# Loads of adaLN weights moved from SyncE's queue to ScalarE's, beside the first FFN product

## The chip, the cores and the metric

The kernel runs on one core of a Trainium2 chip. A core has TensorE (PE, matrix products), VectorE (DVE), ScalarE (ACT), GpSimd (POOL) and SyncE (SP). Each engine works through its own instructions in order and waits for the others on semaphores; 16 DMA engines move data between HBM and on-chip memory. A transfer is started by an instruction on some engine, in that engine's order. The metric is the device time of one execution in microseconds (us), lower is better.

## What is computed

The reference is a two-layer backbone over 1024 latent tokens and 256 context tokens of width 1024. Each layer mixes tokens (attention, long convolution, mLSTM) and then applies a SwiGLU FFN of width 2816. Both are modulated by vectors from a linear map of the condition (adaLN):

```python
for l in range(DEPTH):                                   # DEPTH = 2
    mod = (s_lat @ w_mod[l] + b_mod[l])[:, None, :]       # shift, scale, gate: 6 x 1024 values
    mod_c = s_ctx @ w_mod[l] + b_mod[l]
    ...
    x = x + g1 * y                                        # y: the token mixer
    x = x + g2 * swiglu(modulate(x, norm2_w[l], sh2, sc2), ffn_w_gate[l], ffn_w_up[l], ffn_w_down[l])
    if not last:
        ctx = ctx + g1c * yc
        ctx = ctx + g2c * swiglu(modulate(ctx, ...), ...)
```

## The kernel before, in words

All weights and activations are float32. For TensorE every operand is split in two parts: ScalarE writes a rounded copy ("hi", L137) and VectorE the remainder ("lo", L142), and a product is made of three matmuls: hi by hi, hi by lo, lo by hi.

The stage that the change touches is the first FFN product of layer 0 (`second` calls `up`). It makes gate and up values for 2816 features in 11 pairs of 128-feature blocks, and each pair takes two passes (i = 0 gate, i = 1 up). One such pass, called a step here, computes a 256-feature by 1024-token product with seven half-size products instead of eight (`products`, in the manner of Strassen and Winograd). There are 22 steps. A step's matmuls are 84 of 512 columns (into the PSUM tiles a, b, c, d, lines L1239 to L1241, `partial`) and 48 of 256 columns for the context tokens (into x, lines L169 to L171, the helper `rest` in `up`).

A step needs weights prepared by `up_weights`. Two loads of 512 KB each bring `raw` tiles: one with the quarters A11 and A12, the other with A21 and A22. GpSimd makes four sums of quarters from them (S1, S3, S2, S4, L1176); S1 and S3 need the second tile. ScalarE and VectorE then split the four quarters and the four sums into hi and lo (eight L137 and eight L142 instructions of 128x512). There are two `raw` buffers in all, so a step's loads can start only when the previous step's quarters have been split, and there is one set of split weights, so a split must also wait until TensorE has finished with that tile in the previous step. While TensorE works on a step, the other engines prepare the next one and finish the results of the current one: VectorE combines PSUM tiles (w, y, p, L1176; y is the one that reads b when its second half is done), ScalarE copies (p, L1253 and L1258) and applies SiLU (g), and results go out to `act`.

Beside this stage the kernel makes the rest of the adaLN vectors (`late_mod`), woven into the 22 steps: 160 times a tile `mraw` of 256 KB of adaLN weights is loaded, and one VectorE instruction multiplies it by the SiLU of the condition and sums it (L1739 before, L1737 after; CUSTOM_DVE_ANT_0 in the profile, ISA in the program's rows). There are three `mraw` buffers, so a load waits for the VectorE instruction three tiles earlier. About 7.3 of these fall on a step.

A scheduler sets the order of instructions on each engine, from its own estimate. Tokens constrain it: instructions stamped with one token stay in program order. Before, all loads are issued by SyncE, and the loads of `raw` in the FFN and of `mraw` bear the token "queue".

Of the kernel before, what the change touches and what calls it, by code (L numbers as in the profile page):

```python
# [83 lines left out]
class Kernel:  # L84
# [1190 lines left out]
    def up_weights(self, l, f, i, sp, full):  # L1275

        nc = self.nc
        G = nc.gpsimd
        q, w = {}, {}
        for r in "12":  # L1280
            t = self.t(self.wp, [P, 1024], F32, "raw", 2)
            ins = nc.sync.dma_start(out=t, in_=self.A["wgu"][l, f + int(r) - 1, i])
            self.tc.stamp_issue_order_token(ins.ins, "queue")
            q["A" + r + "1"], q["A" + r + "2"] = t[:, :512], t[:, 512:]
        for x in (("S3", "S4"), ("A11", "A12"), ("S1", "S2"), ("A22", "A21")):
            hi, lo = [self.t(self.wl, [P, 1024], F32R, "w", 8) for _ in range(2)]
            for i, y in enumerate(x):
                w[y] = hi[:, i * 512:(i + 1) * 512], lo[:, i * 512:(i + 1) * 512]
        As, Ss = ("A11", "A12", "A22") + (("A21",) if full else ()), ("S3", "S4", "S1", "S2")
        if sp is None:  # L1290
            for x in As:
                self.split(*w[x], q[x])
            for x, y in (("S1", "A22"), ("S3", "A21"), ("S2", "A11"), ("S4", "A12")):
                q[x] = q[y]
            order = Ss
        else:
            for x in (("S3", "S4"), ("S1", "S2")):
                t = self.t(sp, [P, 1024], F32, "S", bufs=2)
                q[x[0]], q[x[1]] = t[:, :512], t[:, 512:]
            order = Ss[:2] + As[:2] + Ss[2:] + As[2:]  # L1300
        for x, y, z, op in (("S1", "A21", "A22", ALU.add), ("S3", "A11", "A21", ALU.subtract), ("S2", "S1", "A11", ALU.subtract),
                            ("S4", "A12", "S2", ALU.subtract)):
            self.tt(G, q[x], q[y], q[z], op)
        for x in order:
            self.split(*w[x], q[x])
        return w
# [416 lines left out]
    def late_mod(self, mr):  # L1723

        nc = self.nc
        H = DM // 2
        for v, n in ((0, 48), (1, 16)):
            for h in range(2):
                cs = slice(h * H, (h + 1) * H)
                sil = self.t(mr, [P, H], F32, "silb", 1)  # L1730
                nc.sync.dma_start(out=sil, in_=self.A["crow"][v, cs].partition_broadcast(P))
                nc.scalar.activation(out=sil, in_=sil, func=AF.Silu)
                for l, f in [(0, f) for f in range(40, 48)] + [(1, f) for f in range(n)]:
                    d = self.L[l]
                    raw = self.t(mr, [P, H], F32, "mraw", 3)
                    ins = nc.sync.dma_start(out=raw, in_=self.A["wmodT"][l, f][:, cs])
                    self.tc.stamp_issue_order_token(ins.ins, "queue")  # L1737
                    o = d["mod"][:, f, v:v + 1]
                    ins = nc.vector.tensor_tensor_reduce(out=raw, in0=raw, in1=sil, scale=1.0, scalar=o if h else d["bmod"][:, f:f + 1],  # L1739
                                                         op0=ALU.mult, op1=ALU.add, accum_out=o)  # L1740
                    self.tc.stamp_issue_order_token(ins.ins, "pace")
                    yield
# [113 lines left out]
```

## Time and profile before

| what | before |
|---|---|
| device time, median of 3 runs | 3420.31 us (3418.61 to 3427.58) |
| the profiled execution's own time | 3420.54 us |
| its span, first to last instruction | 3418.4 us |
| mean granted TensorE clock | 0.963 of full speed |
| TensorE busy | 3191.8 us, 93% of the span |
| VectorE busy | 2137.8 us, 63% |
| ScalarE busy | 1283.5 us, 38% |
| GpSimd busy | 871.1 us, 25% |
| share of the 16 DMA engines that SyncE's queue took | 41.8% |
| first and last issue of an `mraw` load | 1005.8 us, 1555.1 us |

Times of single instructions are counted from the span's start. A matmul's record overlaps the next one's, so the distance between starts, not the length, is its cost.

### The profile page before, as it was taken

The page shows a single profiled execution, that of the slowest core. Times are in us where ns is not written, and L with a number is a line of the kernel's source. Part 1 is how long each engine was busy: PE and PEld are TensorE (multiplying, and loading weights), DVE is VectorE, ACT ScalarE, POOL GpSimd, SP SyncE. Part 2 cuts the span into 40 slices and gives each one's busy share as a digit, 9 for nine tenths or more (in the row PEclk, how much of TensorE's full clock was granted, in tenths as well). Part 3 has the DMA queues.
Part 4 walks back from the last instruction along what each step waited for, and adds up shares of the span by engine and source line. Part 5 has one row for each costly group of instructions (what it writes and reads, how often), then busy time and mean ns, then how long its engine had stood idle before and what let it go on. Part 6 is the DMA issues. An engine that isn't in the chain of part 4 may idle for free. (4 is left out here: it accounts for less than half of the span.)

```text
span 3418.4 us, 48478 instructions
## 1 busy us (share of the span) xinstructions
PE 3191.8 (93%) x17486; PEld 2737.4 (80%) x17486; DVE 2137.8 (63%) x3929; ACT 1283.5 (38%) x2775; POOL 871.1 (25%) x800
## 2 busy tenths in 40 slices
PE   7998999988979999998999999999899699999998
PEld 3976898887868778787888897899887578887787
DVE  8678457895587766664554755456885844444443
ACT  5544466444352222222221642456344533333210
POOL 2354133111133333332000230133112444443000
PEclk8999999998989999999999999999899899999999
DMA  6676446442624444445331465445336122223432
GB/s 235 204 221 207 121 128 188 138 115 78 199 70 136 139 139 134 157 132 173 106 92 56 131 207 172 129 125 179 102 91 199 62 74 84 77 84 103 159 99 74
DMA packets 350319, 454.48 MB, mean 133 GB/s; under 512 B 48064, under 2 KB 250740, under 8 KB 348287
## 3 DMA queue, kind: packets, MB, share of 16 engines
q1 hardware_dynamic: 349704, 451.05, 41.8%
q8 instruction: 138, 2.26, 0.3%
q14 instruction: 102, 0.84, 0.1%
q10 hardware_dynamic: 375, 0.34, 0.0%
HBM read 335.10 MB, written 116.16 MB: 132 GB/s over the span
## 5 line engine op out<-in xcount | busy, mean ns | idle before, releaser
L137 ACT ACTIVATE w<-raw 128x512 fp32r<-128x512 f32 (+3 forms) x286 | 220.9, 798 | 398.8 <-PE f L170 129.2
L169 PE MATMUL f<-b,w 128*128 128x512 f32 (+1 forms) x912 | 335.3, 377 | 30.9 <-ACT b L137 29.8
L142 DVE TENSOR_TENSOR w<-raw,w 128x512 fp32r<-128x512 f32 (+3 forms) x266 | 268.2, 1025 | 144.9 <-ACT w L137 143.1
L170 PE MATMUL f<-b,w 128*128 128x512 f32 (+1 forms) x912 | 332.7, 366 | 0.0
L171 PE MATMUL f<-b,w 128*128 128x512 f32 (+1 forms) x912 | 331.9, 365 | 0.0
L1374 DVE SCALAR_TENSOR_TENSOR x<-f,mod,x 128x512 f32<-128x512 f32 (+1 forms) x256 | 168.5, 664 | 194.7 <-PE f L171 189.4
L169 PE MATMUL mm<-w,hh 128*128 128x256 f32 (+2 forms) x928 | 279.3, 302 | 9.4 <-ACT hh L315 5.1
L171 PE MATMUL mm<-w,hl 128*128 128x256 f32 (+2 forms) x928 | 276.7, 300 | 5.4 <-DVE hl L316 5.4
L170 PE MATMUL mm<-w,hh 128*128 128x256 f32 (+2 forms) x928 | 277.6, 299 | 1.2 <-DVE w L142 1.2
L142 DVE TENSOR_TENSOR w<-S,w 128x512 fp32r<-128x512 f32 x168 | 136.9, 835 | 155.0 <-ACT w L137 148.1
L169 PEld LDWEIGHTS f<-b,w 128*128 128x128 f32 x912 | 176.1, 195 | 63.5 <-ACT b L137 32.4
L137 ACT ACTIVATE w<-S 128x512 fp32r<-128x512 f32 x168 | 100.5, 624 | 335.0 <-POOL S L1176 331.7
L170 PEld LDWEIGHTS f<-b,w 128*128 128x128 f32 x912 | 175.4, 192 | 29.1 <-DVE b L142 1.0
L171 PEld LDWEIGHTS f<-b,w 128*128 128x128 f32 x912 | 175.0, 192 | 26.5
L169 PEld LDWEIGHTS mm<-w,hh 128*128 128x128 f32 x928 | 178.2, 192 | 14.7 <-ACT hh L315 7.2
L171 PEld LDWEIGHTS mm<-w,hl 128*128 128x128 f32 x928 | 177.1, 192 | 7.3 <-DVE hl L316 6.8
L170 PEld LDWEIGHTS mm<-w,hh 128*128 128x128 f32 x928 | 178.4, 192 | 1.9 <-DVE w L142 1.6
L1239 PE MATMUL d<-hb,w 128*128 128x512 f32 x352 | 142.2, 404 | 15.2 <-ACT w L137 7.7
L1176 POOL TENSOR_TENSOR S<-raw 128x512 f32<-128x512 f32 x42 | 56.1, 1336 | 388.6 <-DMA raw<-in_wgu 328.4
L1241 PE MATMUL b<-hb,w 128*128 128x512 f32 x352 | 139.1, 395 | 12.6 <-DVE w L142 12.6
L1241 PE MATMUL d<-hb,w 128*128 128x512 f32 x352 | 142.6, 405 | 8.9 <-DVE w L142 8.7
L1240 PE MATMUL a<-hb,w 128*128 128x512 f32 x352 | 139.7, 397 | 7.9 <-DVE hb L142 7.8
(697 smaller groups left out, 8815.1 us busy)
## 6 DMA issues: line engine op xcount, KB each, us to landing
raw<-in_wgu SPq DMA_DIRECT2D x88, 512.0 KB
mraw<-in_wmodT SPq DMA_DIRECT2D x160, 256.0 KB
act<-g SPq DMA_DIRECT2D x88, 256.0 KB
raw<-in_wdn SPq DMA_DIRECT2D x44, 512.0 KB
raw<-act SPq DMA_DIRECT2D x42, 512.0 KB
raw<-in_wout SPq DMA_DIRECT2D x32, 512.0 KB
q<-qd SPq DMA_DIRECT2D x144, 96.0 KB
eoL<-eo SPq DMA_DIRECT2D x64, 192.0 KB
```

What stands on the lines that cost most here:

```text
L137: ins = nc.scalar.activation(out=hi, in_=src, func=AF.Copy)
L142: (eng or nc.vector).tensor_tensor(out=lo, in0=src, in1=hi.bitcast(F32), op=ALU.subtract)
L169: nc.tensor.matmul(out=ps, lhsT=ah, rhs=bh, start=(i == 0), stop=False, skip_group_check=on)
L170: nc.tensor.matmul(out=ps, lhsT=ah, rhs=bl, start=False, stop=False, skip_group_check=on)
L171: nc.tensor.matmul(out=ps, lhsT=al, rhs=bh, start=False, stop=(i % part == part - 1 or i == n - 1), skip_group_check=on)
L1176: ins = eng.tensor_tensor(out=out, in0=a, in1=b, op=op)
L1239: nc.tensor.matmul(out=ps, lhsT=ah[:, ks], rhs=bh, start=start and k == 0, stop=False, skip_group_check=not start)
L1240: nc.tensor.matmul(out=ps, lhsT=ah[:, ks], rhs=bl, start=False, stop=False, skip_group_check=not start)
L1241: nc.tensor.matmul(out=ps, lhsT=al[:, ks], rhs=bh, start=False, stop=(k == m - 1), skip_group_check=not start)
L1374: nc.vector.scalar_tensor_tensor(out=x, in0=ps[:, :n], scalar=d["mod"][:, 40 + m, v:v + 1], in1=x, op0=ALU.mult, op1=ALU.add)
```

## The change

`late_mod` issues the `mraw` loads from ScalarE instead of SyncE. Both loads lose the token "queue". Nothing that is computed changes.

```diff
@@ up_weights
             t = self.t(self.wp, [P, 1024], F32, "raw", 2)
-            ins = nc.sync.dma_start(out=t, in_=self.A["wgu"][l, f + int(r) - 1, i])
-            self.tc.stamp_issue_order_token(ins.ins, "queue")
+            nc.sync.dma_start(out=t, in_=self.A["wgu"][l, f + int(r) - 1, i])
@@ late_mod
                     raw = self.t(mr, [P, H], F32, "mraw", 3)
-                    ins = nc.sync.dma_start(out=raw, in_=self.A["wmodT"][l, f][:, cs])
-                    self.tc.stamp_issue_order_token(ins.ins, "queue")
+                    nc.scalar.dma_start(out=raw, in_=self.A["wmodT"][l, f][:, cs])
```

The rows that follow are of one step in the middle of the stage, whose `raw` tiles are raw_2342 (A11, A12) and raw_2343 (A21, A22). In brackets stands what a row waits for: DMAHW is an earlier transfer's arrival, the others are instructions of the engine named. First SyncE, before; mraw_2335 to mraw_2341 are adaLN tiles.

```order
L1736 DMA mraw_2335_12018<-in_wmodT 128x512 [waits DMAHW6_49,DVE_49]
L1736 DMA mraw_2336_12034<-in_wmodT 128x512 [waits DMAHW7_49,DVE_49]
L1731 DMA silb_2334_12015<-in_crow 128x512 [waits DMAHW0_49,DVE_49]
L1736 DMA mraw_2337_12049<-in_wmodT 128x512 [waits DMAHW1_49]
L1736 DMA mraw_2338_12067<-in_wmodT 128x512 [waits DMAHW2_49,DVE_49]
L1736 DMA mraw_2339_12083<-in_wmodT 128x512 [waits DMAHW3_49,DVE_49]
L1736 DMA mraw_2341_12145<-in_wmodT 128x512 [waits DMAHW4_49,DVE_49]
L1282 DMA raw_2342_12148<-in_wgu 128x1024 [waits DMAHW5_49,Activation_49,Pool_49]
L1282 DMA raw_2343_12150<-in_wgu 128x1024 [waits DMAHW6_49,Activation_49]
```

SyncE in the changed kernel; raw_2313 is the second tile of the step before.

```order
L1282 DMA raw_2313_11931<-in_wgu 128x1024 [waits DMAHW2_49,DMAHW0_49,DVE_49]
L1282 DMA raw_2342_12148<-in_wgu 128x1024 [waits DMAHW3_49,DMAHW7_49,DVE_49,Pool_49]
L1730 DMA silb_2334_12015<-in_crow 128x512 [waits DMAHW2_49,DVE_49]
L1282 DMA raw_2343_12150<-in_wgu 128x1024 [waits DMAHW3_49,DMAHW0_49,DVE_49]
L1340 DMA act3_1860_8860<-g_2305_11867 128x512 [waits DMAHW7_49,DVE_49]
L1340 DMA act3_1860_8860<-g_2306_11868 128x512 [waits DMAHW1_49,Pool_49]
```

The loads of the step's weights stood behind the `mraw` loads, which wait for VectorE; now only the silb load stands between them, and each waits for its own buffer.

Now ScalarE around the same step, before (w is the hi part; S_2352 holds S3 and S4, S_2353 holds S1 and S2).

```order
L1258 ACTIVATE p1_2324_11963<-a_2328_11967 128x512 [waits PE_49]
L137 ACTIVATE w_2344_12152<-S_2352_12160 128x512 [waits PE_49,Pool_49]
L137 ACTIVATE w_2346_12154<-raw_2342_12148 128x512 [waits DMAHW5_49,PE_49]
L137 ACTIVATE w_2346_12154<-raw_2342_12148 128x512
L137 ACTIVATE w_2348_12156<-S_2353_12161 128x512 [waits PE_49]
L137 ACTIVATE w_2348_12156<-S_2353_12161 128x512 [waits Pool_49]
L137 ACTIVATE w_2350_12158<-raw_2343_12150 128x512 [waits DMAHW6_49,DVE_49,PE_49]
L137 ACTIVATE w_2350_12158<-raw_2343_12150 128x512
L137 ACTIVATE w_2344_12152<-S_2352_12160 128x512 [waits Pool_49]
```

ScalarE in the changed kernel.

```order
L1735 DMA mraw_2338_12067<-in_wmodT 128x512 [waits DMAHW4_49,DVE_49]
L1258 ACTIVATE p1_2324_11963<-a_2328_11967 128x512 [waits PE_49]
L137 ACTIVATE w_2344_12152<-S_2352_12160 128x512 [waits Pool_49] x2
L1735 DMA mraw_2339_12083<-in_wmodT 128x512 [waits DMAHW5_49,DVE_49]
L1735 DMA mraw_2341_12145<-in_wmodT 128x512 [waits DMAHW6_49,DVE_49]
L137 ACTIVATE w_2346_12154<-raw_2342_12148 128x512 [waits DMAHW7_49,PE_49]
L137 ACTIVATE w_2346_12154<-raw_2342_12148 128x512
L1735 DMA mraw_2362_12203<-in_wmodT 128x512 [waits DMAHW0_49,DVE_49]
L137 ACTIVATE w_2348_12156<-S_2353_12161 128x512 [waits PE_49]
L137 ACTIVATE w_2348_12156<-S_2353_12161 128x512
L1735 DMA mraw_2363_12231<-in_wmodT 128x512 [waits DVE_49]
L1735 DMA mraw_2364_12247<-in_wmodT 128x512 [waits DMAHW4_49,DVE_49]
```

The hi of S4, last before, comes right behind that of S3. Five `mraw` loads, each of which waits for VectorE, stand ahead of splits of this step (those of raw_2343 come next), and one stands ahead of the copy p of a.

Last VectorE, before: the rows from the last results of the step under way to the first lo of the next (w_2345 is the lo of S3).

```order
L1176 TENSOR_TENSOR g_2305_11867<-a_2328_11967,g_2305_11867 128x512 [waits PE_49]
L1176 TENSOR_TENSOR y__2327_11966<-b_2329_11968,p1_2324_11963 128x512 [waits PE_49]
L1176 TENSOR_TENSOR p1_2324_11963<-c_2330_11969,y__2327_11966 128x512 [waits DVE_49]
L1739 ISA mraw_2338_12067,mod0_315<-mraw_2338_12067,silb_2334_12015,mod0_315 128x512 [waits DMAHW2_49]
L1739 ISA mod0_315 128x1
L1176 TENSOR_TENSOR w__2326_11965<-d_2331_11970,w__2326_11965 128x512 [waits PE_49]
L1739 ISA mraw_2339_12083,mod0_315<-mraw_2339_12083,silb_2334_12015,mod0_315 128x512 [waits DMAHW3_49]
L1739 ISA mod0_315 128x1
L1739 ISA mraw_2341_12145,mod0_315<-mraw_2341_12145,silb_2334_12015,mod0_315 128x512 [waits DMAHW4_49]
L1739 ISA mod0_315 128x1
L142 TENSOR_TENSOR w_2345_12153<-S_2352_12160,w_2344_12152 128x512 [waits Activation_49]
L1176 TENSOR_TENSOR g_2307_11869<-w__2326_11965,g_2307_11869 128x512 [waits DVE_49]
```

VectorE in the changed kernel.

```order
L142 TENSOR_TENSOR w_2345_12153<-S_2352_12160,w_2344_12152 128x512 [waits Activation_49]
L1176 TENSOR_TENSOR g_2305_11867<-a_2328_11967,g_2305_11867 128x512 [waits PE_49]
L1176 TENSOR_TENSOR y__2327_11966<-b_2329_11968,p1_2324_11963 128x512 [waits PE_49]
L142 TENSOR_TENSOR w_2347_12155<-raw_2342_12148,w_2346_12154 128x512 [waits DMAHW7_49,Activation_49]
L1176 TENSOR_TENSOR p1_2324_11963<-c_2330_11969,y__2327_11966 128x512 [waits DVE_49]
L1737 ISA mraw_2338_12067,mod0_315<-mraw_2338_12067,silb_2334_12015,mod0_315 128x512 [waits DMAHW4_49]
L1737 ISA mod0_315 128x1
L1176 TENSOR_TENSOR w__2326_11965<-d_2331_11970,w__2326_11965 128x512 [waits PE_49]
L1737 ISA mraw_2339_12083,mod0_315<-mraw_2339_12083,silb_2334_12015,mod0_315 128x512 [waits DMAHW5_49]
L1737 ISA mod0_315 128x1
```

The last lo of the S3 and S4 pair now stands ahead of y, where before the first one stood behind y and three adaLN instructions. TensorE's order changes with it: a step starts with its 12 matmuls into d and 12 into c without the hops between tiles that it made before.

## Rows read from the trace of the kernel before

**Rows 1.** Busy time of each engine in two stretches, then TensorE's clock and DMA.

```profile
1001.00:1020.00 19.00, 8.37 (x35) 7.06 (x36) 16.72 (x38) 9.90 (x23) 2.64 (x2) 0.64 0.36 108
...
1048.35:1562.52 514.17, 486.88 (x2507) 406.34 (x2506) 348.97 (x548) 131.38 (x239) 184.09 (x117) 1.00 0.44 140
```

**Rows 2.** VectorE's timeline: y of steps 2 and 21 (start, us, instruction).

```profile
1048.35 0.69 DVE L1176 TENSOR_TENSOR y__2140_10676<-b,p 128x512 f32<-128x512 f32 x1 [2.29 <-PE b L1241]
...
1562.52 0.69 DVE L1176 TENSOR_TENSOR y__2732_14768<-b,p 128x512 f32<-128x512 f32 x1 [6.82 <-PE b L1241]
```

**Rows 3.** TensorE's timeline, matmuls that follow each other without a wait.

```profile
1503.42 0.39 PE L1239 MATMUL b<-hb,w 128*128 128x512 f32 x1
...
1506.14 0.40 PE L1239 MATMUL d<-hb,w 128*128 128x512 f32 x1
...
1507.55 0.28 PE L169 MATMUL x<-hc,w 128*128 128x256 f32 x1
...
1513.29 0.49 PE L1239 MATMUL d<-hb,w 128*128 128x512 f32 x1
```

**Rows 4.** Waits of TensorE, 1020 to 1600 us: total, times, longest.

```profile
PE b L1241 <- DVE w L142: 12.6, 9, 1.7
PE d L1241 <- DVE w L142: 6.2, 11, 1.2
PE a L1241 <- DVE w L142: 4.3, 9, 0.8
PE d L1239 <- ACT w L137: 3.2, 4, 1.0
```

**Rows 5.** GpSimd's timeline: first sum of four steps.

```profile
1183.87 1.29 POOL L1176 TENSOR_TENSOR S<-raw 128x512 f32<-128x512 f32 x1 [15.56 <-DMA raw<-in_wgu]
...
1212.24 1.57 POOL L1176 TENSOR_TENSOR S<-raw 128x512 f32<-128x512 f32 x1 [20.26 <-DMA raw<-in_wgu]
...
1238.79 1.29 POOL L1176 TENSOR_TENSOR S<-raw 128x512 f32<-128x512 f32 x1 [15.26 <-DMA raw<-in_wgu]
...
1560.80 1.29 POOL L1176 TENSOR_TENSOR S<-raw 128x512 f32<-128x512 f32 x1 [12.55 <-DMA raw<-in_wgu]
```

**Rows 6.** VectorE's timeline around two steps.

```profile
1196.20 1.28 DVE L142 TENSOR_TENSOR w<-raw,w 128x512 fp32r<-128x512 f32 x2
...
1202.57 0.75 DVE L1739 CUSTOM_DVE_ANT_0 mraw<-mraw,silb,mod 128x512 f32<-128x512 f32 x1
...
1209.31 0.69 DVE L1176 TENSOR_TENSOR y__2327_11966<-b,p 128x512 f32<-128x512 f32 x1 [4.42 <-PE b L1241]
...
1226.49 1.28 DVE L142 TENSOR_TENSOR w<-raw,w 128x512 fp32r<-128x512 f32 x2
```

**Rows 7.** SyncE's queue, timeline: issue of three steps' loads.

```profile
1203.79 0.84 SPq L1282 DMA_DIRECT2D raw<-in_wgu  x2
...
1231.04 0.86 SPq L1282 DMA_DIRECT2D raw<-in_wgu  x2
...
1555.48 0.86 SPq L1282 DMA_DIRECT2D raw<-in_wgu  x2
```

**Rows 8.** Waits of SyncE's queue, 1005 to 1600 us: total, times, longest.

```profile
SPq L1736 <- DVE mod L1739: 375.7, 150, 12.4
```

**Rows 9.** GpSimd's groups, 1048.35 to 1562.52 us: busy us, mean ns.

```profile
L1176 POOL TENSOR_TENSOR S<-raw,S 128x512 f32<-128x512 f32 x19 | 32.8, 1724 | 0.2
```

**Rows 10.** Instructions on tile mraw: ns minimum/median/maximum, first and last start.

```profile
L1736 SPq DMA_DIRECT2D mraw<-in_wmodT x160: 327/328/817, 1005.8 to 1555.1; - x160
...
L1739 DVE CUSTOM_DVE_ANT_0 mraw<-mraw,silb,mod x80: 733/743/1800, 1200.0 to 1567.4; 128x512 f32<-128x512 f32 x80
```

**Rows 11.** ScalarE's groups, 1048.35 to 1562.52 us: busy, mean ns, idle before.

```profile
L137 ACT ACTIVATE w<-S 128x512 fp32r<-128x512 f32 x76 | 45.3, 624 | 240.0 <-POOL S L1176 239.9
```

**Rows 12.** TensorE's timeline: the first context matmul of the stage.

```profile
1009.43 0.58 PE L169 MATMUL x<-hc,w 128*128 128x256 f32 x1 [7.35 <-ACT hc L137]
```

**Rows 13.** ScalarE's timeline at the same place: SiLU of the condition.

```profile
1011.79 0.63 ACT L1732 ACTIVATE silb<-silb 128x512 f32<-128x512 f32 x1
```

## Prediction

> **What bounds the kernel now.** I read the busy times by stretch first. Between y of step 2 and y of step 21 [rows 2] lie 514.17 us, 19 steps of 27.06 us each, and TensorE is busy for 486.88 us of them at full clock [rows 1]. That share says little, since records overlap, so I counted a step's own work from matmuls that follow each other without a wait [rows 3]: 12 into b take 2.72 us (0.227 each), 6 into d take 1.41 us (0.235), 48 into x take 5.74 us (0.120). A step has 60 matmuls into a, b and c, 24 into d and 48 into x: 13.6 + 5.6 + 5.7 = 25.0 us, to a tenth. TensorE thus loses about 2.1 us per step. Its waits say for what: 26.3 us in four rows, nearly all for a lo on VectorE or a hi on ScalarE [rows 4], and each restart costs some more. So TensorE is starved of split weights, a little in every step.
>
> Where do these come late from? GpSimd's sums start when the loads arrive (its waits for `raw` are 15 to 20 us long [rows 5]), and the loads are issued late. I followed two steps round. The lo of the second `raw` tile end at 1196.20 + 1.28 = 1197.5 and 1226.49 + 1.28 = 1227.8 [rows 6]; from then on the buffers are free. The next loads are issued at 1203.79 and 1231.04 [rows 7], 6.3 and 3.3 us later. In the first case an adaLN instruction starts at 1202.57 and ends after 0.75 us [rows 6]; an `mraw` load stands ahead of the step's loads in SyncE's queue and waits for it. SyncE waited 375.7 us in 150 waits of this kind [rows 8]. The loads arrive, by GpSimd's start, at 1212.24 and 1238.79 [rows 5], 8.4 and 7.8 us after issue. From arrival to the last lo it takes 13.6 us (1183.87 to 1197.5) and 15.5 us (1212.24 to 1227.8).
>
> That is a closed loop, since there is one step's worth of buffers: prepare, wait in the queue, travel, prepare. 13.6 + 6.3 + 8.4 = 28.3 and 15.5 + 3.3 + 7.8 = 26.6, mean 27.5, against 27.06 measured over 19 steps. So the loop sets the pace now, not TensorE's 25.0.
>
> **The change, part by part.** *The wait in the queue* (6.3 and 3.3, mean 4.8 us a step) goes: SyncE no longer stands behind `mraw`. What remains ahead of the second tile's load are writes of results, whose data are ready before its buffer is.
>
> *The travel.* The first `raw` tile is freed some instructions earlier than the second and its load is now issued by itself, so the load that closes the loop is the last 512 KB alone. The bounds are the shortest of the stage, 1555.48 to 1560.80, 5.3 us [rows 5, 7], and the longest followed here, 8.4 us. I take 6.0, near the short end, since half the data is already under way.
>
> *The preparation gets longer.* In the changed order the lo of S4 comes ahead of y, and the step's own results follow behind it; before, y, p, w and three adaLN instructions ran while VectorE waited for the loads. From arrival: four sums on GpSimd, 1.29 us each when VectorE is quiet [rows 5] and 1.72 when it isn't [rows 9], so 5.2 to 6.9; I take 5.6, because VectorE then mostly waits for TensorE. The hi of S4 is 0.62 us [rows 11], its lo 0.64 (half of the pair in [rows 6]). Then up to the last lo of the second tile: 11 instructions of about 0.6 us between starts and 5 adaLN ones of 0.74 [rows 10], 10.3 us, or two short ones less in every other step, 9.1. Three GpSimd results in one kind of step, and one in the other, run beside them; beside GpSimd an adaLN instruction has taken up to 1.80 us instead of 0.74 [rows 10], so each adds about 1.1 us: 13.6 and 10.2, mean 11.9. Sum of the new loop: 6.0 + 5.6 + 1.3 + 11.9 = 24.8 us. With every bound at its high end it is 8.4 + 6.9 + 1.3 + 13.6 = 30.2, with every one at its low end 5.3 + 5.2 + 1.3 + 9.1 = 20.9.
>
> At 24.8 the loop is level with TensorE's 25.0. Two chains of one length that wait for each other don't reach either exactly; I take 25.5 us a step, half a microsecond over the longer. The 20 steps after the first then gain 20 x (27.06 - 25.5) = 31 us. If TensorE alone set the pace they would gain 41.
>
> *ScalarE issues 160 loads.* On SyncE one took 0.33 us, at most 0.82 [rows 10]; the trace has none on ScalarE. 160 x 0.33 = 53 us, 160 x 0.82 = 131 us. ScalarE is busy for 131 of 514 us [rows 1] and idles 240 us before splits of sums alone [rows 11], so either fits; below zero it cannot be. Cost taken: nothing. Two or three issues stand ahead of splits that VectorE uses soon; were they bare, they would cost 1 us a step, 20 us in all.
>
> *ScalarE waits for VectorE.* A load queued on ScalarE waits for the adaLN instruction three tiles back. Behind it stand the splits and the copies p of a and d, and TensorE may not add to a and d before these are made. By the rows of the changed order, the load ahead of p of a waits for an adaLN instruction that follows the last lo, some 13 to 14 us after the lo of S4; TensorE needs that p 19 us after y (x 5.7, d 2.8, c, a and b 2.7 each, 10 of d 2.3). Covered by some 4 us, so nothing; the rival below prices it.
>
> *The start of the stage.* TensorE waited 7.35 us for the context's hi [rows 12]. In the new order the later ones stand behind loads that wait for the first adaLN instructions, and these for the SiLU at 1011.79 [rows 13]. Three adaLN instructions of 0.74 come first: 2.2 us, less if other work is at hand, and twice that if the issues delay them too. I take 2 (0 to 4).
>
> *The rest.* Layer 1 has no `mraw`, and its order differs in a few rows that swap: nothing. Later stages shift as a whole.
>
> Sum: 31 - 2 = 29 us off the profiled execution's 3420.54 us, which is 0.2 us over the median: 3391.5; I give 3392.
>
> **The rivals.** *The gain is given back (no change).* The queue's 4.8 us go, but the results that move behind the lo of S4 fill VectorE as long: y, p and w at 0.6, three adaLN instructions at 0.74, two GpSimd collisions of 1.1, together 6.2 us. If the travel stays at the two cases' mean of 8.1 us, the loop is 24.8 + 2.1 = 26.9, a gain of 3 us, less 2 at the start: 3419. For it speaks that the two lengths are near; against it that half the load is under way earlier and that the sums now fall where VectorE waits.
>
> The Trainium skill's page DMA: Bandwidth & Descriptors (Issuing engines are not separate DMA queues) speaks for this rival: loads from several engines interleave on the same 16 DMA engines, and a second issuer saves only the issuing time. The trace agrees that SyncE's issue is short, 0.33 us [rows 10]; but what this change removes is a wait at the head of a queue, which the rule does not count, and which rows 8 show. By the rule alone the time would stay at 3420.
>
> *ScalarE is held up (slower).* If the last lo of a step comes over 18 us after y instead of 13 to 14, the load ahead of p of a holds p past the point at which TensorE needs it, TensorE stalls, y of the next step comes later, and the loop closes through ScalarE. It decides from there on. With the loop's high end less the collisions that can't all coincide, 30.2 - 1.6 = 28.6 us, the steps lose 1.5 us: 20 x 1.5 + 2 = 32, so 3453. For it: five waits on VectorE stand between a step's splits on an engine that had none. Against it: all of them wait for VectorE instructions that stand earlier than the lo that uses the split behind them.
>
> *TensorE sets the pace (faster still).* If the travel takes 5.3 us and GpSimd's sums 5.2, the loop is 23.7 and waits vanish: 41 - 0 = 41, so 3379.
>
> **Chances and range.** The forecast's case, 3381 to 3408, has 0.44; TensorE's pace, 3374 to 3381, 0.14; the gain given back, 0.20; ScalarE held up, 0.22. 0.3%, about 10 us, is what a measurement of this kernel can tell from no change. Faster by more than that: the first two, and a quarter of the third, 0.63. Within: 0.17, of the third nearly all that is left and a little of the last. Slower: 0.20. For 8 in 10 the range reaches below to TensorE's pace, 3377, and above to part of the slow case, 3432, and so leaves out the bounds at which all the unknown costs are high at once.
>
> **What would show it.** In the changed profile a step's loads should be issued within 1 us of the last lo of the tile whose buffer they take, the two apart from each other; GpSimd's first sum should come before y of the step, not after; the distance from y to y should be 25 to 26 us; TensorE's waits for lo and hi, 26.3 us now, should fall under 8. Waits of ScalarE on the adaLN result should be many, but end before TensorE asks for a p. The prediction is wrong if y to y stays at 27 with VectorE never waiting (given back), or if TensorE's waits name p or a hi on ScalarE that stands behind an adaLN load (held up).

## The result, and the profile after

The changed kernel takes 3388.18 us (median of 4 runs, 3384.43 to 3391.16), the kernel before 3423.94 us (4 runs, 3418.61 to 3432.76): a ratio of 0.9889, 95% interval 0.987 to 0.9909, so 1.1% faster. The forecast was 3392. The profiled execution took 3384.43 us with a span of 3382.6 us, 36.1 us and 35.8 us less than before.

First the y of steps 1, 2, 21 and 22 on VectorE's timeline of the changed kernel (start, us, instruction, idle before).

```profile
1029.13 0.69 DVE L1176 TENSOR_TENSOR y__2105_10457<-b,p 128x512 f32<-128x512 f32 x1 [0.99 <-PE b L1241]
...
1051.67 0.69 DVE L1176 TENSOR_TENSOR y__2140_10676<-b,p 128x512 f32<-128x512 f32 x1 [2.29 <-PE b L1241]
...
1526.41 0.69 DVE L1176 TENSOR_TENSOR y__2732_14768<-b,p 128x512 f32<-128x512 f32 x1 [0.46 <-PE b L1241]
...
1558.15 0.68 DVE L1176 TENSOR_TENSOR y__2778_15056<-b,p 128x512 f32<-128x512 f32 x1
```

The same four before; the middle two are known from [rows 2].

```profile
1026.60 0.69 DVE L1176 TENSOR_TENSOR y__2105_10457<-b,p 128x512 f32<-128x512 f32 x1 [7.72 <-PE b L1241]
...
1594.71 0.68 DVE L1176 TENSOR_TENSOR y__2778_15056<-b,p 128x512 f32<-128x512 f32 x1
```

From step 2 to 21 there are now 474.74 us, 19 steps of 24.99 us, against 27.06. That is the 25.0 us that was counted as TensorE's own work. Balance: y of step 1 comes 2.5 us later; from it to y of step 22 it takes 529.0 us instead of 568.1, which gives 39.1; what follows takes 0.8 us more; what is left of the 39.1 is the span's 35.8.

The windows of the same stretches as in [rows 1] (busy us of PE, PEld, DVE, ACT, POOL, then TensorE's clock, DMA share, GB/s):

```profile
1001.00:1020.00 19.00, 5.07 (x19) 4.17 (x19) 17.28 (x34) 10.74 (x23) 7.31 (x6) 0.59 0.32 97
...
1051.67:1526.41 474.74, 474.74 (x2509) 409.11 (x2508) 311.07 (x548) 137.78 (x240) 174.44 (x115) 1.00 0.46 151
```

TensorE is busy without a gap. Its waits from 1020 to 1600 us, which before held 26.3 us for split weights [rows 4], are down to one row, and that one lies in the next stage:

```profile
PE f L169 <- ACT b L137: 6.3, 1, 6.3
```

Now the loop, at about the step that [rows 5 to 7] showed. SyncE's queue, the issues of one step's two loads:

```profile
1182.23 0.33 SPq L1282 DMA_DIRECT2D raw<-in_wgu  x1
...
1186.85 0.33 SPq L1282 DMA_DIRECT2D raw<-in_wgu  x1
```

VectorE: the lo of the tiles whose buffers they take, and y of the step.

```profile
1181.47 0.68 DVE L142 TENSOR_TENSOR w<-raw,w 128x512 fp32r<-128x512 f32 x1
...
1185.53 1.29 DVE L142 TENSOR_TENSOR w<-raw,w 128x512 fp32r<-128x512 f32 x2
...
1201.59 0.69 DVE L1176 TENSOR_TENSOR y__2327_11966<-b,p 128x512 f32<-128x512 f32 x1 [1.98 <-PE b L1241]
```

GpSimd: the first sum from these loads.

```profile
1191.66 1.30 POOL L1176 TENSOR_TENSOR S<-raw 128x512 f32<-128x512 f32 x1 [12.62 <-DMA raw<-in_wgu]
```

The last lo of the second tile ends at 1186.82 and its load is issued 0.03 us later; before, that took 6.3 and 3.3 us. It is so in every step: from the last lo of a step to the next load it takes 2.3 to 7.3 us before, mean 4.6 over 20 steps, and 0.02 to 0.04 us now. The two loads stand 4.6 us apart. From issue to first sum it is 4.8 us (4.1 to 6.3 over the 20 steps, mean 5.1) instead of 8.4 and 7.8, and the first sum begins 9.9 us before y, where before it began after y (1212.24 against 1209.31, [rows 5, 6]).

ScalarE's groups between y of step 2 and of step 21 (busy us, mean ns, idle before and what ended it), and the new issues (ns minimum/median/maximum):

```profile
L137 ACT ACTIVATE w<-S 128x512 fp32r<-128x512 f32 x76 | 45.9, 628 | 156.0 <-POOL S L1176 117.3 <-PE x L171 25.0 <-DMA mraw<-in_wmodT 7.8
L137 ACT ACTIVATE w<-raw 128x512 fp32r<-128x512 f32 x77 | 44.4, 624 | 64.2 <-PE b L1240 39.8 <-DVE mod L1737 22.1 <-PE x L170 1.1
L1253 ACT ACTIVATE p<-d 128x512 f32<-128x512 f32 x19 | 11.4, 599 | 31.8 <-DVE mod L1737 24.9 <-PE d L1241 5.7 <-DVE w L142 1.2
L1258 ACT ACTIVATE p<-a 128x512 f32<-128x512 f32 x19 | 11.4, 599 | 72.9 <-PE a L1241 49.8 <-DMA mraw<-in_wmodT 21.9 <-DVE mod L1737 1.2
```

```profile
L1735 ACTq DMA_DIRECT2D mraw<-in_wmodT x160: 334/334/1163, 1005.4 to 1521.3; - x160
```

ScalarE does wait for the adaLN result (DVE mod) ahead of splits and of p, 48.2 us in these rows (22.1 + 24.9 + 1.2), and another 29.7 us (7.8 + 21.9) for the arrival of adaLN tiles. No matmul waits for it.

### The profile page after: what moved, and what is told of

Read it like the earlier page. It is cut to its first block, busy times and chain, and to the rows that moved or that the text cites. A ratio compares the mean times of both kernels' runs of the same rounds, so it can differ in the third digit from the quotient of the medians.

```text
span 3382.6 us, 48435 instructions
## 1 busy us (share of the span) xinstructions
PE 3183.2 (94%) x17486; PEld 2744.0 (81%) x17486; DVE 2091.9 (62%) x3929; ACT 1292.5 (38%) x2775; POOL 857.4 (25%) x800
## 5 line engine op out<-in xcount | busy, mean ns | idle before, releaser
L142 DVE TENSOR_TENSOR w<-raw,w 128x512 fp32r<-128x512 f32 (+3 forms) x266 | 239.3, 914 | 157.7 <-ACT w L137 155.7
L169 PE MATMUL mm<-hh,w 128*128 128x512 f32 (+1 forms) x360 | 144.5, 401 | 0.0
```

The source lines that it names most:

```text
L142: (eng or nc.vector).tensor_tensor(out=lo, in0=src, in1=hi.bitcast(F32), op=ALU.subtract)
L169: nc.tensor.matmul(out=ps, lhsT=ah, rhs=bh, start=(i == 0), stop=False, skip_group_check=on)
```

## The experiments

With the loads on ScalarE and both tokens kept, the scheduler makes the changed kernel's program, instruction for instruction on every engine. So once ScalarE issues, the tokens do nothing. The opposite was run.

**The tokens alone** (tokens_only). Both loads stay on SyncE.

```diff
             t = self.t(self.wp, [P, 1024], F32, "raw", 2)
-            ins = nc.sync.dma_start(out=t, in_=self.A["wgu"][l, f + int(r) - 1, i])
-            self.tc.stamp_issue_order_token(ins.ins, "queue")
+            nc.sync.dma_start(out=t, in_=self.A["wgu"][l, f + int(r) - 1, i])
...
-                    ins = nc.sync.dma_start(out=raw, in_=self.A["wmodT"][l, f][:, cs])
-                    self.tc.stamp_issue_order_token(ins.ins, "queue")
+                    nc.sync.dma_start(out=raw, in_=self.A["wmodT"][l, f][:, cs])
```

> Both loads lose their token, and both stay on SyncE. Written order on VectorE and TensorE becomes nearly that of the changed kernel; in SyncE's queue the adaLN loads stand between the loads of a step, in the order in which the scheduler expects their buffers to come free. Theory of the engine (the step's loads must not stand behind adaLN loads at all): a wait of some 2 us a step stays in the queue, steps take 26 to 27 us, time 3405 to 3420. Theory of the order (only the place of the loads in the queue mattered, and the token froze it): the step's loads wait for their own buffers, steps take 25.0 us, time 3383 to 3392, and the move to ScalarE was not needed.

Measured: 3391.84 us, ratio 0.9905 (0.9885 to 0.9925), and 24.98 us a step: the whole gain, without ScalarE. SyncE's queue waits nearly as long as before (375.7 us in [rows 8]):

```profile
SPq L1735 <- DVE mod L1737: 348.3, 133, 11.1
```

Its timeline at the step above, then VectorE's:

```profile
1191.28 0.42 SPq L1735 DMA_DIRECT2D mraw<-in_wmodT  x1
1192.10 0.33 SPq L1282 DMA_DIRECT2D raw<-in_wgu  x1
1197.20 0.33 SPq L1735 DMA_DIRECT2D mraw<-in_wmodT  x1
```

```profile
1190.79 1.29 DVE L142 TENSOR_TENSOR w<-raw,w 128x512 fp32r<-128x512 f32 x2
```

The lo ends at 1192.08 and the load goes at 1192.10: the adaLN load ahead of it had left at 1191.28, and the next one, which waits till 1197.20, stands behind it. So it was not the queue shared with adaLN loads that cost time, nor SyncE's waiting, but that the token put the step's loads behind adaLN loads whose buffers come free later.

**Another issuer** (pool_issue).

```diff
-                    nc.scalar.dma_start(out=raw, in_=self.A["wmodT"][l, f][:, cs])
+                    nc.gpsimd.dma_start(out=raw, in_=self.A["wmodT"][l, f][:, cs])
```

> As the changed kernel, but GpSimd issues the adaLN loads. If it is only SyncE's queue that mattered and the issuer is free, steps take 25.0 us as with ScalarE, 3383 to 3392, and ScalarE's waits on the adaLN result are gone. Rival: the issuing engine matters, since GpSimd's sums stand in the loop and now wait behind adaLN loads, each of which waits for VectorE: sums begin 2 to 5 us later, steps take 26 to 28 us, 3405 to 3450.

Measured: 3389.18 us, ratio 0.9898 (0.9877 to 0.9919), 25.00 us a step. GpSimd waits much, from 1020 to 1560 us, and TensorE for none of it:

```profile
POOL mraw L1735 <- DVE mod L1737: 134.7, 85, 4.2
POOL S L1176 <- DMA raw<-in_wgu: 51.1, 20, 6.0
```

Three issuers give one time. The Trainium skill's page DMA: Bandwidth & Descriptors (Issuing engines are not separate DMA queues) says that a second issuer saves only the issuing time, and these three runs agree with it; the gain came from the place in the program, of which that rule does not speak.

**Less work for TensorE** (before_shortpe and after_shortpe): the same edit in both kernels leaves out 32 of a step's 48 context matmuls, which by [rows 3] are 32 x 0.120 = 3.8 us.

```diff
-                self.mm3(ps[:, r * 256:(r + 1) * 256],
-                         [(tuple(t[:, k % 4 * P:(k % 4 + 1) * P] for t in w[f"A{r + 1}{k // 4 + 1}"]), hc[k]) for k in range(KB)])
+                for k in range(KB):
+                    nc.tensor.matmul(out=ps[:, r * 256:(r + 1) * 256], lhsT=w[f"A{r + 1}{k // 4 + 1}"][0][:, k % 4 * P:(k % 4 + 1) * P],
+                                     rhs=hc[k][0], start=(k == 0), stop=(k == KB - 1))
```

> The kernel before with 32 of a step's 48 context matmuls left out (hi by lo and lo by hi), so that TensorE's own work per step falls from 25.0 to 21.2 us. If the loop of buffer, queue, travel and preparation sets the pace, steps still take 26 to 27 us. If TensorE sets it together with its waits, they take 27.06 - 3.8 = 23.2 us.

> The changed kernel with the same 32 matmuls per step left out. The pace then shows how long the loop is without TensorE in the way. My sum says 24.8 us, so steps would shrink little, to 24 to 25 us. If the loop is shorter (the one followed in the trace of the changed kernel, from one arrival to the next, took 22.9 us with TensorE's waits in it), they take 21.5 to 23 us.

Measured, one execution each: 3407.99 and 3323.73 us. y of steps 2 and 21, before without these matmuls:

```profile
1056.90 0.69 DVE L1176 TENSOR_TENSOR y__2140_10644<-b,p 128x512 f32<-128x512 f32 x1 [2.03 <-PE b L1241]
...
1562.18 0.68 DVE L1176 TENSOR_TENSOR y__2732_14128<-b,p 128x512 f32<-128x512 f32 x1
```

And of the changed kernel without them:

```profile
1059.85 0.68 DVE L1176 TENSOR_TENSOR y__2140_10644<-b,p 128x512 f32<-128x512 f32 x1
...
1484.70 0.68 DVE L1176 TENSOR_TENSOR y__2732_14128<-b,p 128x512 f32<-128x512 f32 x1
```

In the first, TensorE's longest row of waits from 1020 to 1600 us, and its window between these two y:

```profile
PE d L1239 <- ACT w L137: 67.1, 21, 6.7
```

```profile
1056.90:1562.18 505.28, 435.31 (x1908) 353.37 (x1907) 332.52 (x549) 134.68 (x244) 179.43 (x119) 0.94 0.44 141
```

3.8 us less work per step shorten the step before by only 0.5 us, from 27.06 to 26.59, and TensorE waits for a hi instead: its pace came from the loop. (Its granted clock was 0.94 there and not 1.00, and its busy time fell by 2.7 us a step, from 25.6 to 22.9, and not by 3.8; that is still far more than the step did.) In the changed kernel the step falls by 2.6 us, to 22.36, so its loop is that long at most, not 24.8. (The scheduler's order shifts a little with such an edit; in the changed kernel the loads still go within 0.14 us of their buffers' release.)

**VectorE's order** (lo_in_order). The changed kernel, with the eight lo of a step given the token "pace" of VectorE's other results (hc says that the context is computed too, as in this stage).

```diff
-        (eng or nc.vector).tensor_tensor(out=lo, in0=src, in1=hi.bitcast(F32), op=ALU.subtract)
+        ins = (eng or nc.vector).tensor_tensor(out=lo, in0=src, in1=hi.bitcast(F32), op=ALU.subtract)
+        if pace:
+            self.tc.stamp_issue_order_token(ins.ins, "pace")
...
-            self.split(*w[x], q[x])
+            self.split(*w[x], q[x], pace=sp is not None and hc)
```

> The changed kernel, but the eight lo of a step are bound to VectorE's other results of the stage in program order. VectorE then has the order of before: the first lo stands behind y, p, w and three adaLN instructions; the loads keep their free place. If the queue ahead of the loads was the loss, steps take 25.0 to 25.5 us and the time is 3383 to 3400. Rival: the loss was VectorE's order, and the free loads only let the lo move ahead of y; then steps take 26.5 to 27 us, 3410 to 3425.

Measured: 3389.7 us, ratio 0.9905 (0.9889 to 0.992); 24.95 us a step but for one of 29.31 (last section). VectorE's timeline, y and the first lo behind it:

```profile
1202.45 0.69 DVE L1178 TENSOR_TENSOR y__2327_11966<-b,p 128x512 f32<-128x512 f32 x1 [2.10 <-PE b L1243]
...
1208.47 1.28 DVE L142 TENSOR_TENSOR w<-S,w 128x512 fp32r<-128x512 f32 x2
```

The first lo stands behind y again, as before, and the gain is the same; so the gain does not come from lo that move ahead of y. VectorE's order is not that of before in all: the lo of S4 comes second of the eight, not last. TensorE's order differs from before in the changed kernel, in tokens_only and here, and no run holds it as it was; that it plays no part is not shown.

**Fewer adaLN buffers**, in the kernel before (before_mraw2) and in the changed one (after_mraw2, after_mraw1). The third is the edit with 1.

```diff
-                    raw = self.t(mr, [P, H], F32, "mraw", 3)
+                    raw = self.t(mr, [P, H], F32, "mraw", 2)
```

> The kernel before with two adaLN buffers instead of three. SyncE's queue then waits for VectorE's instruction two tiles back instead of three, so a step's loads, which stand behind these, wait longer: by about one adaLN instruction and what lies between two of them, 0.7 to 2 us a step. If the queue ahead of the loads closes the loop, steps take 27.8 to 29 us, 3436 to 3465. If the queue's wait is not in the loop, nothing changes, 3415 to 3430, as nearly nothing changed with two buffers where ScalarE issues.

> The changed kernel with two adaLN buffers instead of three: each load on ScalarE waits for VectorE's instruction two tiles back, and the splits and copies behind it wait longer. If the cover that I counted ahead of TensorE's need for p (some 4 us) is there, steps take 25.0 to 25.5 us, 3383 to 3400. If ScalarE has no slack left, TensorE's waits name p or a hi, steps take 26 to 28 us, 3405 to 3450.

> The changed kernel with one adaLN buffer: each load on ScalarE waits for the instruction on the tile just before, and each instruction for its own load's whole travel. It is to show where ScalarE's slack ends. If the waits behind adaLN loads can hold up ScalarE as my slower rival said, TensorE's waits now name p and hi, and steps take 28 to 35 us, 3450 to 3600. If ScalarE and VectorE still keep up, 25 to 26 us, 3385 to 3410.

Measured with two buffers: before 3556.14 us, ratio 1.0373 (1.0349 to 1.0397), 33.2 us a step; changed 3388.39 us, ratio 0.99 (0.988 to 0.992), 25.15 us a step. So the wait in the queue is in the loop; I had expected 27.8 to 29 us, and had its size wrong by far. VectorE's timeline of before with two buffers shows why:

```profile
1246.90 1.28 DVE L142 TENSOR_TENSOR w<-raw,w 128x512 fp32r<-128x512 f32 x2
...
1262.10 0.69 DVE L1176 TENSOR_TENSOR y__2327_11966<-b,p 128x512 f32<-128x512 f32 x1 [4.64 <-PE b L1241]
...
1263.44 1.34 DVE L1739 CUSTOM_DVE_ANT_0 mraw<-mraw,silb,mod 128x512 f32<-128x512 f32 x1
```

And SyncE's queue:

```profile
1264.82 0.33 SPq L1736 DMA_DIRECT2D mraw<-in_wmodT  x1
1265.25 0.85 SPq L1282 DMA_DIRECT2D raw<-in_wgu  x2
```

The buffers are free at 1248.18; the loads go at 1265.25, 17.1 us later. The adaLN load ahead of them now waits for an adaLN instruction that stands behind y, and y waits for TensorE's product of the step. Loads, splits and matmuls follow each other where they should overlap. Over 20 steps the loads wait 15.1 us on average, against 4.6 with three buffers. TensorE's granted clock was 0.90 between y of steps 2 and 21, and its busy time 26.9 us a step instead of 25.6, which is 1.3 of the 6.1 us:

```profile
1065.88:1696.27 630.39, 510.74 (x2499) 431.79 (x2498) 339.20 (x548) 132.81 (x239) 170.36 (x115) 0.90 0.35 116
```

With one buffer in the changed kernel (3516.34 us, one execution) the step is 32.3 us, and the slower rival is there, with a granted clock of 0.93. ScalarE's longest row of waits from 1000 to 1600 us, and TensorE's:

```profile
ACT w L137 <- DVE mod L1737: 212.5, 40, 16.2
```

```profile
PE x L169 <- ACT w L137: 35.2, 12, 4.4
```

**Twice the issues on ScalarE** (after_halves).

```diff
-                    nc.scalar.dma_start(out=raw, in_=self.A["wmodT"][l, f][:, cs])
+                    for j in range(2):
+                        nc.scalar.dma_start(out=raw[:, j * H // 2:(j + 1) * H // 2], in_=self.A["wmodT"][l, f][:, h * H + j * H // 2:h * H + (j + 1) * H // 2])
```

> The changed kernel with each adaLN tile loaded in two halves: 320 issues on ScalarE instead of 160, 160 x 0.33 = 53 us more of them, the same bytes. If issues on ScalarE cost nothing here, the time stays within 0.2% of the changed kernel's, 3382 to 3395. If they are bare, it rises by up to 53 us, 3410 to 3441.

Measured: 3393.99 us, ratio 0.9918 (0.99 to 0.9936), 5.8 us over the changed kernel's median, with intervals that overlap. The profile settles it for the stage: from y of step 1 (1042.81) to y of step 22 (1571.58) it takes 528.8 us, against 529.0 with half the issues. Issues cost nothing here.

**The start of the stage** (after_take8, after_first8). In the first the adaLN work begins after step 1; in the second SyncE issues the first eight loads.

```diff
-                    weave((up, 16 * NFF // 2), (self.late_mod(mr), 168))
+                    list(self.take(up, 8))
+                    weave((up, 16 * NFF // 2 - 8), (self.late_mod(mr), 168))
```

```diff
-                    nc.scalar.dma_start(out=raw, in_=self.A["wmodT"][l, f][:, cs])
+                    (nc.sync if k < 8 else nc.scalar).dma_start(out=raw, in_=self.A["wmodT"][l, f][:, cs])
+                    k += 1
```

> The changed kernel, but the adaLN work starts after the first step, so that the context's hi no longer stand behind adaLN loads at the stage's start. If those loads cost the start its 2.5 to 3.3 us, y of step 2 comes by that much earlier after the first context matmul, and the time is 3380 to 3388. Rival: the start is bound by the norm that feeds the hi, and nothing changes, 3384 to 3392; or the adaLN work that is pushed into 21 steps fills VectorE and a step takes 25.3 us, 3390 to 3397.

> The changed kernel, but the first eight adaLN loads are issued by SyncE, which has nothing else to do there; ScalarE issues the others. If loads on ScalarE hold the context's hi at the stage's start, the first context matmul to y of step 1 takes 17.2 us again instead of 18.9, and the time falls by 2 to 3 us, 3383 to 3388. Rival: the start is bound elsewhere and nothing changes, 3386 to 3391.

Measured: 3388.56 us, ratio 0.9902 (0.9887 to 0.9917), and 3389.58 us, ratio 0.989 (0.9871 to 0.9908): no difference that the times can tell. In the traces, the first context matmul to y of step 2 takes 38.9 us before, 41.4 changed, 39.1 with the adaLN work later, 42.4 with SyncE's issues. So ScalarE's queue is not what costs the start 2.5 us: it is lost where the adaLN work is there, whoever issues its loads. But before had the same work there and did not lose it. What is new is that GpSimd's sums for step 2 run beside it, since that step's loads went at 976.25 us and not at 1019.29 (GpSimd is busy for 7.31 us from 1001 to 1020 us, before for 2.64 [rows 1]). VectorE before, and GpSimd's first of these sums:

```profile
1012.46 0.75 DVE L1739 CUSTOM_DVE_ANT_0 mraw<-mraw,silb,bmod 128x512 f32<-128x512 f32 x1 [0.89 <-ACT silb L1732]
```

```profile
1026.15 1.30 POOL L1176 TENSOR_TENSOR S<-raw 128x512 f32<-128x512 f32 x1 [21.98 <-DMA raw<-in_wgu]
```

VectorE in the changed kernel:

```profile
1012.57 1.59 DVE L1737 CUSTOM_DVE_ANT_0 mraw<-mraw,silb,bmod 128x512 f32<-128x512 f32 x1 [1.31 <-ACT silb L1731]
...
1014.09 1.74 DVE L1737 CUSTOM_DVE_ANT_0 mraw<-mraw,silb,bmod 128x512 f32<-128x512 f32 x1
```

GpSimd:

```profile
1012.34 1.26 POOL L1176 TENSOR_TENSOR S<-S,raw 128x512 f32<-128x512 f32 x1
1013.68 1.60 POOL L1176 TENSOR_TENSOR S<-raw,S 128x512 f32<-128x512 f32 x1
```

TensorE, which waits for the lo of the context behind these:

```profile
1016.90 0.58 PE L170 MATMUL x<-hc,w 128*128 128x256 f32 x1 [2.64 <-DVE hc L142]
```

The first three adaLN instructions took 0.75 us each before, and 1.59, 1.74 and 0.74 now, where the third has no sum beside it; with SyncE's issues two of them took 1.74. That is 1.8 us of the 2.5; what makes up the rest is open.

No variant that does the same work has a lower median than the changed kernel.

## Why the prediction was right, and which step was off

The forecast held in time, and in mechanism as to what bounded the kernel before and what the change removes. What it had wrong is the pace that is left: TensorE alone sets it, which was the rival "TensorE sets the pace", given a chance of 0.14. The forecast gain, 29 us, was 7 short of the profiled execution's 36.1. That 3392 is only 4 us off is in part luck: the median of the kernel before was 3423.94 here, 3.6 over the one that the forecast started from.

- *A loop through the weight buffers sets the pace, not TensorE.* Shown: with 3.8 us less for TensorE the step before shortens by 0.5 us, and a longer wait in the queue lengthens it to 33.2.
- *The wait in the queue goes.* Right: 0.02 to 0.04 us in 20 steps. But the reason given was too wide. I took SyncE's 375.7 us of waits as a sign of the loss; 348.3 us of them stayed in tokens_only at no cost. What counted was only which loads stood behind a waiting one. And ScalarE was not needed for it.
- *The travel, 6.0 us.* 4.8 in the step followed, 5.1 on average: a little long, for the right reason (the load that closes the loop goes alone).
- *The preparation grows to 18.8 us and the loop to 24.8, level with TensorE, so 25.5 us a step.* This is the step that failed. after_shortpe bounds the loop by 22.36 us: 5.2 of travel and 17.2 from arrival to the last lo, on average, with what is left of TensorE's waits in it. There is a slack of at least 2.6 us, TensorE alone sets the pace, and the steps take 24.99 us. The term "20 x (27.06 - 25.5) = 31" should have been 20 x 2.07 = 41, as the rival "TensorE sets the pace" had it for this term; from y of step 2 to y of step 22 the gain is 39.9, since the last step gains only 0.45. That the lo move ahead of y, on which the 18.8 rested, was not even needed: lo_in_order has them behind it and takes as long.
- *ScalarE's issues cost nothing.* Right: 0.33 us each as on SyncE, and twice as many left the stage as long.
- *ScalarE's waits are covered.* Right with three buffers; with two a step grows by 0.16 us, with one the rival comes true.
- *The start costs 2 us.* 2.5 from the first context matmul on, the right size by luck. I blamed loads ahead of the context's hi; after_first8 rules out ScalarE's queue. The three adaLN instructions that I counted at 2.2 us stood there before as well; what was added is GpSimd's sums beside them.
- *The rest of the kernel, nothing.* 0.8 us after step 22, and 0.8 ahead of the first context matmul (1010.24 us against 1009.43). With the start's 2.5 they take the 39.9 down to the span's 35.8; that rival had all three at nothing, so its 3379 was too low.

The rival that nothing would change put the travel at 8.1 us and the loop at 26.9. Both came out shorter, 5.1 and at most 22.36. The results that it counted do run inside the preparation (y at 1201.59, after the arrival at 1191.66); the whole is just not as long as it summed.

## What to carry to other kernels

A long total of queue waits says nothing by itself; look for the load whose buffer is free while it stands behind one that still waits, and measure that gap (here 4.6 us a step against 0.03). Where a scheduler may order the loads by when their buffers come free, a token that fixes program order across two streams can cost what a second queue seems to save. To know which chain sets the pace, and how much slack the other has, shorten one of them: 3.8 us off TensorE moved one kernel by 0.5 us a step and the other by 2.6.

## What the runs showed of the hardware

One step of lo_in_order took 4.4 us more than the others after less than 2 us without work for TensorE. ScalarE waited for one load of the condition (silb) that SyncE had issued late, with a hi behind it (timeline of ScalarE):

```profile
1458.39 0.63 ACT L1734 ACTIVATE silb<-silb 128x512 f32<-128x512 f32 x1 [9.09 <-DMA silb<-in_crow]
```

The windows of these microseconds (columns as above):

```profile
1458.00:1460.00 2.00, 0.93 (x5) 0.39 (x3) 0.95 (x3) 1.61 (x3) 0.00 (x0) 1.00 0.87 335
1460.00:1462.00 2.00, 1.18 (x5) 0.69 (x4) 2.00 (x5) 1.83 (x5) 0.00 (x0) 0.86 0.49 128
1462.00:1464.00 2.00, 2.00 (x6) 1.62 (x5) 2.00 (x4) 0.42 (x1) 0.00 (x0) 0.50 0.63 225
1464.00:1466.00 2.00, 2.00 (x8) 1.59 (x7) 2.00 (x5) 0.60 (x1) 0.00 (x0) 0.79 0.86 241
```

TensorE was busy for 2.1 of 4 us, and then its granted clock was 0.50, the lower level (1.2 of 2.4 GHz), for 2 us and more. Here a gap of 1.9 us stands in a step that lost 4.4.

Issuing a load took GpSimd 0.54 us, against 0.33 on SyncE and ScalarE:

```profile
L1735 POOL DMA_DIRECT2D mraw<-in_wmodT x160: 538/538/761, 1002.6 to 1522.5; - x160
```

And y of step 1 came between 1026.60 and 1042.81 us in profiles of programs that hardly differ ahead of it, while the mean step lies between 24.98 and 25.00 us in the changed kernel, tokens_only, pool_issue, after_halves, after_take8 and after_first8. In these six y of step 1 spreads over 15 us (1027.96 to 1042.81), and what follows it to the end of the span over 5 (2350.5 to 2355.4): most of the spread between these executions is made ahead of y of step 1.
